# Gates behind the attention by tanh, one request for the Ln/Exp table moved, and a longer planned trip for the recurrence's first unit

## The chip, the cores and the metric

The kernel runs on one core of a Trainium2 chip. The metric is the device time of one launch in microseconds; of several runs the median counts. The core's engines are TensorE (PE; PEld are its weight loads), VectorE (DVE), ScalarE (ACT), GpSimd (POOL) and SyncE (SP), which here issues DMAs.

## The reference

One block of a hybrid model on a sequence of 1024 rows and 1024 columns in fp32: a modulated RMS norm, one wide projection, softmax attention with forget gates (8 heads of 64) beside an RWKV-7 recurrence (8 heads of 64), both weighted by sigmoid gates, an output projection, a second norm, a convolutional FFN (2816) and a last norm.

```python
def token_mixer(u, w_in, fox_b_f, fox_w_out, rwkv_mu, ...):
    proj = u @ w_in
    p_fox, p_rwkv, p_gate = _split(proj, (FOX_COLS, RWKV_COLS, GATE_COLS))
    ...
    o_fox = fox_attention(to_heads(q), to_heads(k), to_heads(v), log_f)
    o_rwkv = rwkv7_time_mix(p_rwkv, ...)
    gate_fox, gate_rwkv = jnp.split(jax.nn.sigmoid(p_gate), N_BRANCHES, axis=-1)
    merged = gate_fox * (o_fox @ fox_w_out) + gate_rwkv * (o_rwkv @ rwkv_w_out)
    return merged @ w_o

def reference(x, c, ...):
    mod = jax.nn.silu(c) @ w_mod[l] + b_mod[l]
    shift1, scale1, gate1, shift2, scale2, gate2 = jnp.split(mod, N_MOD, axis=-1)
    u = modulate(rms_norm(h, ln1_g[l]), shift1, scale1)
    h = h + gate1[:, None, :] * token_mixer(u, ...)
    u = modulate(rms_norm(h, ln2_g[l]), shift2, scale2)
    h = h + gate2[:, None, :] * conv_ffn(u, ...)
    return rms_norm(h, final_g)
```

## The kernel before, in words

Every fp32 operand of a product is split into a high and a low part (`hi_in`, `lo_in`, `u_hi`, `u_lo`), and a product is the sum of three: high by high, low by high, high by low. ScalarE casts the high part, VectorE or GpSimd subtracts for the low one. A projection of 128 columns is two halves (`hf`) of the 1024 rows, each of 3 x 8 matmuls of 128 x 512.

The program has these stages. The *start* squares and transposes `x` (`xt`), sums the modulation from the rows of `w_mod` (`wm`) and makes `u`. Then come low-rank products (*lora*) and the first projections. The *recurrence* goes over 8 units (pair of heads `p`, half `hf`): a preparation (`pre`) inverts small triangular matrices on VectorE (rows `t` and `E`), and a main part (`main`) turns the result `TT` into `X`, multiplies (`xi`, `zi`) and passes a state `S` through eight chunks, each by a TensorE product `sp` and a VectorE scaling. The *attention* follows (`lg` logits, `P` probabilities, `tp` their transpose, `th` and `tl` its parts, `ov` the product with the values); its results are `fx0` (high) and `fx1` (low). Then come the *branch* products (`br`, x = 0 from attention and 1 from recurrence, with weights `raw_br`, `hi_br`, `lo_br`), multiplied by the gates (`g`) on VectorE, the output projection (`wo`), the second norm (`norm2`, once for each half of the rows) and the FFN. During `br`, VectorE also adds up two more modulation vectors from `wm` tiles (`acc3`, `acc4`) and splits the recurrence's results (`rk_raw`) into high and low.

TensorE's order is written by a planner, `Weave`: it keeps a clock `now` from the modelled cost of each matmul, runs chains that yield times to wait, and fills the gaps with steps of projections from a queue: `qk`, `v`, `rkv` and last the 16 gates (`gt`, `gs`). While the attention runs, DVE's and ACT's orders are written out as well; elsewhere the scheduler of the language orders them. Gates taken up before the attention run through `gate_steps` in the form Abs, Exp, Ln, a subtraction and Exp. Gates taken up in it (`weave.late` is 1) run through `late_gate` and `gate_out`, which use 0.5 tanh(0.5 x) + 0.5 and the PSUM tile `rk_ps`; what is left in the queue when `weave.late` is 2 runs behind the attention in the form of `gate_steps` again. The `big` PSUM pool has 2 banks, a pool of loaded weights (`raw`) 2 tiles; `br` goes round 4 banks.

For the first unit, `ready` is the planner's time at which the inverse is back from VectorE and two DMAs: `now` plus 47500 ns; the other units have 38500. `main` waits for `ready - 1500` before it lays out the transposes of X.

`use_ln_exp(after)` asks ScalarE to load the table set that holds Ln and Exp, and with `after` it is ordered behind that instruction; without it, nothing ties it to a place. `rms_rstd` (L292, L293) is an Ln and an Exp.

Of the kernel before, what the change touches and what calls it, by code (L numbers as in the profile page):

```python
# [11 lines left out]
AF = mybir.ActivationFunctionType  # L12
# [123 lines left out]
def hybrid_block(ctx: ExitStack, tc: tile.TileContext, a, out):  # L136
    nc = tc.nc
    weave = Weave()
# [43 lines left out]
    epsr = cp.tile([128, 4], F32, name="epsr")  # L182
# [20 lines left out]
    def use_ln_exp(after=None):  # L203

        i = nc.scalar.preload_act_table_set("natural_log_exp_and_others")
        if after is not None:
            tc.add_manual_dep(i.ins, after.ins.name, NOSYNC)


    d_gate = dr.tile([16, 128, S], F32, name="d_gate")  # L210
# [41 lines left out]
    marks = {}  # L252
# [26 lines left out]
    def gemm_steps(ps, w, x, cs, nk=KT, w0=0, by_kt=False):  # L279
        (wh, wl), (xh, xl) = w, x  # L280
        order = [(i, kt) for i in range(3) for kt in range(nk)]
        if by_kt:
            order.sort(key=lambda o: o[1])
        for n, (i, kt) in enumerate(order):
            ww, xx = ((wh, xh), (wh, xl), (wl, xh))[i]
            k0 = (w0 + kt) * 128
            mm(ps, ww[:, k0 : k0 + 128], xx[:, kt, cs], start=n == 0, stop=n == len(order) - 1)
            yield
# [32 lines left out]
    def gate_steps(w, i, pps, ptag, pool, tag):  # L321
        if weave.late == 1:
            yield from late_gate(w, i)
            return
        for hf in range(2):
            cs = slice(hf * NH, hf * NH + NH)
            ps = pps.tile([128, NH], F32, tag=ptag, name=f"gt{i}_{hf}")
            yield from gemm_steps(ps, w, u, cs)

            g = pool.tile([128, NH], F32, tag=tag, name=f"gs{i}_{hf}")  # L330
            nc.scalar.activation(g, ps, AF.Abs)
            nc.scalar.activation(g, g, AF.Exp, scale=-1.0)
            nc.scalar.activation(g, g, AF.Ln, bias=1.0)
            stt(g, ps, 0.0, g, op0=ALU.min, op1=ALU.subtract)
            nc.scalar.activation(g, g, AF.Exp)
            nc.sync.dma_start(d_gate[i, :, cs], g)
# [3 lines left out]
    with ExitStack() as es:  # L340
# [7 lines left out]
        def gen(name):  # L348
            return pr.tile([128, NH], F32, tag="gen", name=name)
# [407 lines left out]
        def pre(k, p, hf):  # L757

            n = f"{p}_{hf}"
            cs = slice(hf * NH, hf * NH + NH)  # L760
# [5 lines left out]
            def chunk_tile(nm, bufs, *dims):  # L766
                return rw.tile([128, *dims], F32, tag=nm, name=f"{nm}{n}", bufs=bufs)
# [46 lines left out]
            for c0 in range(0, NCU, 4):  # L814
                ps = [gen(f"p1_{n}{h}{c0}") for h in range(2)]
# [15 lines left out]
            M32 = chunk_tile("M32", 1, 32, 32)  # L831
            for g in range(4):
                nc.sync.dma_start(M32[g * 32 : g * 32 + 32, :, :], sm.rearrange("h c b s t -> (h c b) s t"))
            ready = weave.now + (47500 if k == 0 else 38500)
            TT = chunk_tile("TT", 2, NCU, CH)
            weave.spawn(inverse(n, M32, TT, chunk_tile, tmp), 8500)

# [12 lines left out]
            ps = [gen(f"tb{n}{h}") for h in range(2)]  # L850
# [144 lines left out]
        for i in range(16):  # L995
            weave.add(lambda i=i: w_in(26 + i), lambda w, i=i: gate_steps(w, i, pb, "big", gsp, "sp0"))
# [4 lines left out]
        def pre_chain():  # L1001
            for k, (p, hf) in enumerate(order):
                while got[p, hf] < 3:
                    weave.step()
                yield from pre(k, p, hf)
                if p < 3:
                    weave.first.extend(rkv_items(p + 1, hf))
                yield 0
# [43 lines left out]
    with tc.manual_schedule(engines={mybir.EngineType.DVE, mybir.EngineType.Activation}):  # L1052
# [170 lines left out]
        def late_gate(w, i):  # L1223
            for hf in range(2):
                cs = slice(hf * NH, hf * NH + NH)
                yield from gemm_steps(rk_ps, w, u, cs)
                weave.hold = weave.now + 700
                pending.append((i, hf))
                weave.spawn(gate_out(i, hf, cs), 260)
                yield  # L1230

        def gate_out(i, hf, cs):

            g = gsp.tile([128, NH], F32, tag="sp0", name=f"gs{i}_{hf}")
            nc.scalar.activation(g, rk_ps, AF.Tanh, scale=0.5)
            weave.hold = weave.use("ACT", weave.now, 480) + 210
            nc.scalar.activation(g, g, AF.Identity, scale=0.5, bias=epsr[:, 3:4])
            weave.use("ACT", weave.now, 480)
            nc.sync.dma_start(d_gate[i, :, cs], g)
            pending.remove((i, hf))  # L1240
            return
            yield

        def drain():
            begun = weave.cur
            while pending or (weave.cur is begun and begun is not None):
                yield 300
# [2 lines left out]
        weave.run([a_chain(), t_chain(), s_chain()])  # L1250
        weave.late = 2
        weave.run([drain()])
    use_ln_exp()
    es.close()
    pz = ctx.enter_context(tc.tile_pool(name="pz", bufs=1, space=PS))

    def bank(k, name):
        return pb.tile([128, NH], F32, tag="big", name=name) if k > 5 else pz.tile([128, NH], F32, tag=f"p{k}", name=name)
# [33 lines left out]
    br_open(0, 1)  # L1292
    while weave.step():
        pass
    u_st.close()
    ww_st.close()
    pools["m"] = ctx.enter_context(tc.tile_pool(name="sm", bufs=1, side="right", reuse_waits="tile"))
# [75 lines left out]
    for x in range(2):  # L1373
        for n in range(8):
            if x or n:
                k = 8 * x + n + 1
# [299 lines left out]
    ps = {t: [bank(k, f"wo{t}_{c}") for c, k in enumerate(ks)] for t, ks in enumerate(((0, 5), (6, 7), (1, 2)))}  # L1676
# [12 lines left out]
    def wo_do(t, k):  # L1689
        ps = [bank(k + c, f"wo{t}_{c}") for c in range(2)]  # L1690
        for kt in range(KT):
            wo_mm(t, kt, ps)
        return ps

    ps = wo_do(3, 3)
# [5 lines left out]
    ps = wo_do(4, 0)  # L1701
# [11 lines left out]
    for t, k in ((5, 2), (6, 6), (7, 4)):  # L1713
        ps = wo_do(t, k)
# [223 lines left out]
    for s, k in enumerate(ORDER):  # L1938
        ps = banks[4:] if k in (7, 4, 2) else banks[0:4]
# [109 lines left out]
```

## Time and profile before

| | us |
|---|---|
| median of 3 runs | 1674.13 |
| lowest and highest run | 1671.78, 1674.92 |
| profiled execution | 1671.68 |
| its span, first to last instruction | 1669.9 |

The mean granted TensorE clock was 0.989. Stages by their times in the trace: start to 60, lora and first projections to 215, first unit of the recurrence to 262, the other units to 620, attention to 824.6, then gate 15 and, from 835.5, `br` (to 923), output projection, second norm and FFN to the end. In the rows of the trace a line has start, duration, engine, source line, operation, written tile <- read tiles, shape, and in brackets how long the engine had stood idle and on what it waited. L144 is the helper through which all matmuls go. TensorE's last `ov` ends at 822.80.

### The profile page before, as it was taken

The numbers are of one execution on the slowest core, as the hardware profiler recorded it, in microseconds if no ns is written. First come the engines' busy times: TensorE is split into PE (matmuls) and PEld (weight loads), VectorE is DVE, ScalarE is ACT, GpSimd is POOL, SyncE is SP. The second block draws the span as 40 slices with busy tenths as digits, with TensorE's granted clock in tenths as the row PEclk, the third lists the DMA queues.
The fourth block names the chain that finished last, engine by engine and source line by source line (L and its number), as shares of the span: only waits on it lengthen the run. The fifth ranks groups of instructions, "written<-read, shape, count | busy, mean of one in ns | idle before, by whom it ended". The sixth has DMA issues, their size and how long they took to land.

```text
span 1669.9 us, 25913 instructions
## 1 busy us (share of the span) xinstructions
PE 1617.1 (97%) x9722; PEld 1322.9 (79%) x9722; DVE 1208.5 (72%) x2357; ACT 814.8 (49%) x1475; POOL 136.2 (8%) x169
## 2 busy tenths in 40 slices
PE   6899999999999999999999999999999999999998
PEld 4677877787987777787788888888888888888886
DVE  5786787887876636777578445897777777786677
ACT  6463343534355556666533244654444444455455
POOL 0010101211111020222122000000000000000000
PEclk7899999999999999999999999999999999999999
DMA  8497745543343237443387420143323323574463
GB/s 334 136 326 223 186 125 134 130 113 94 105 118 94 87 110 172 127 140 99 117 288 262 171 77 38 64 132 108 101 95 104 111 95 107 194 271 153 129 211 108
DMA packets 121853, 241.70 MB, mean 145 GB/s; under 512 B 39816, under 2 KB 48320, under 8 KB 121728
## 3 DMA queue, kind: packets, MB, share of 16 engines
q1 hardware_dynamic: 112896, 220.94, 41.1%
q0 software_dynamic: 7600, 17.25, 3.8%
q10 hardware_dynamic: 1232, 1.86, 0.4%
q8 instruction: 76, 1.25, 0.3%
q14 instruction: 49, 0.40, 0.1%
HBM read 174.43 MB, written 65.56 MB: 144 GB/s over the span
## 4 chain that ended last, share of the span: by engine, by line
PE 80%; DVE 10%; ACT 5%; DMA 2%; issue 2%; SPq 0%; ACTq 0%; DVEq 0%
PE X L144 13%; PE D L144 13%; PE gt L144 7%; PE Y L144 6%; PE ps_rkv L144 6%; PE br L144 5%; PE wo L144 5%; PE qk L144 4%; PE W L144 3%; PE v L144 3%; PE rk_ps L144 2%; DVE nm L1090 1%; PE low L144 1%; PE ov L144 1%; PE sp L144 1%
## 5 line engine op out<-in xcount | busy, mean ns | idle before, releaser
L144 PE MATMUL D<-op,op 128*128 128x512 f32 x924 | 209.8, 389 | 0.0
L144 PEld LDWEIGHTS D<-op,op 128*128 128x128 f32 x924 | 173.3, 188 | 36.3 <-DVE op L1312 0.3
L144 PE MATMUL X<-T_m,S 128*128 128x512 f32 x440 | 107.4, 390 | 0.1
L144 PEld LDWEIGHTS X<-T_m,S 128*128 128x128 f32 x440 | 82.4, 188 | 18.3 <-ACT T_m L1737 0.7
L1311 ACT CAST op<-g 128x512 fp32r<-128x512 f32 x77 | 47.8, 621 | 73.8 <-PE D L144 47.6
L1312 DVE TENSOR_TENSOR op<-g,op 128x512 fp32r<-128x512 f32 x77 | 53.0, 688 | 41.5 <-ACT op L1311 41.5
L268 DVE TENSOR_TENSOR lo_in<-raw_in,hi_in 128x512 fp32r<-128x512 f32 x96 | 65.9, 724 | 23.5 <-ACT hi_in L263 12.2
L1548 DVE SCALAR_TENSOR_TENSOR c<-ab,vec,c 128x512 f32<-128x512 f32 x88 | 65.9, 750 | 19.5 <-ACT c L1551 17.9
L263 ACT CAST hi_in<-raw_in 128x1024 fp32r<-128x1024 f32 x48 | 50.2, 1049 | 46.5 <-PE ps_rkv L144 27.0
L1512 DVE TENSOR_TENSOR S<-ur,S 128x512 fp32r<-128x512 f32 x66 | 45.4, 690 | 35.4 <-ACT S L1508 35.2
L1163 DVE TENSOR_TENSOR tl<-tp,th 128x512 fp32r<-128x512 f32 (+1 forms) x80 | 50.4, 632 | 27.9 <-ACT th L1158 27.2
L1508 ACT CAST S<-ur 128x512 fp32r<-128x512 f32 x66 | 41.1, 623 | 55.6 <-DVE ur L1501 30.6
L1512 DVE TENSOR_TENSOR A<-ur,A 128x512 fp32r<-128x512 f32 x64 | 44.0, 687 | 31.2 <-ACT A L1508 31.0
L738 DVE TENSOR_TENSOR t<-E,M 128x60 f32<-128x60 f32 (+24 forms) x248 | 55.8, 225 | 10.9 <-DMA M<-sm 4.6
L144 PE MATMUL Y<-T_h,A 128*128 128x512 f32 x264 | 63.5, 389 | 0.0
L144 PE MATMUL Y<-T_h,S 128*128 128x512 f32 x264 | 63.3, 389 | 0.0
L742 DVE TENSOR_TENSOR E<-E,t 128x60 f32<-128x60 f32 (+24 forms) x248 | 56.8, 229 | 5.8
L144 PE MATMUL X<-B_b,A 128*128 128x512 f32 x252 | 60.8, 390 | 0.0
L1099 ACT ACTIVATE P<-lg,nm 128x896 f32<-128x896 f32 (+3 forms) x64 | 47.5, 743 | 27.0 <-DVE nm L1090 24.7
L144 PE MATMUL W<-B_f,A 128*128 128x512 f32 x252 | 60.6, 389 | 0.0
L144 PEld LDWEIGHTS Y<-T_h,A 128*128 128x128 f32 x264 | 49.6, 188 | 10.4
L144 PEld LDWEIGHTS Y<-T_h,S 128*128 128x128 f32 x264 | 49.5, 188 | 10.3
(486 smaller groups left out, 4062.7 us busy)
## 6 DMA issues: line engine op xcount, KB each, us to landing
raw_in<-in_w_in SPq DMA_DIRECT2D x50, 512.0 KB
wm<-in_w_mod SPq DMA_DIRECT2D x48, 512.0 KB
ur<-in_w_up SPq DMA_DIRECT2D x44, 512.0 KB
g<-d_g SPq DMA_DIRECT2D x35, 512.0 KB
d_g<-gs SPq DMA_DIRECT2D x44, 256.0 KB
d_g<-c SPq DMA_DIRECT2D x33, 256.0 KB
d_st<-qh SPq DMA_DIRECT2D x64, 128.0 KB
d_gate<-gs SPq DMA_DIRECT2D x32, 256.0 KB
```

The costliest lines, as they stand in the source:

```text
L144: weave.last = nc.tensor.matmul(o, lhsT, rhs, start=start, stop=stop, skip_group_check=more)
L263: nc.scalar.copy(hi, raw)
L268: nc.vector.tensor_tensor(lo[:, c : c + NH], raw[:, c : c + NH], f32(hi[:, c : c + NH]), op=ALU.subtract)
L738: i = tt(tv, E32[:, 0:J, s : s + 1].to_broadcast([128, J, W]), M32[:, s : s + 1, s + 1 : 32].to_broadcast([128, J, W]), op=ALU.mult)
L742: tt(E32[:, 0:J, s + 1 : 32], E32[:, 0:J, s + 1 : 32], tv, op=ALU.add)
L1099: nc.scalar.activation(e[:, 0:n], lg[:, 0:n], AF.Exp, bias=nm[:, 0:1], accum_out=total)
L1163: tt(tl[:, 0:w], tp[:, 0:w], f32(th[:, 0:w]), op=ALU.subtract)
L1311: nc.scalar.copy(hi, src)
L1312: tt(lo, src, f32(hi), op=ALU.subtract)
L1508: nc.scalar.copy(hi, src)
L1512: tt(lo, src, f32(hi), op=ALU.subtract)
L1548: stt(c, ab[:, x + hf * NH : x + hf * NH + NH], V("conv_w", 22 * x + i), c, op0=ALU.mult, op1=ALU.add)
```

## The change

The diff has four parts. `gate_steps` gets a tanh branch for `weave.late` 2, the same arithmetic as in `gate_out`. The first unit's `ready` goes from 47500 to 51500 ns ahead. The bare `use_ln_exp()` behind the attention is taken out, and one is put behind the loop that empties the queue, ordered behind the last gate's second activation, which `gate_out` and the new branch note in `marks["gate"]`.

```diff
--- before.py
+++ after.py
@@ -328,6 +328,11 @@
             yield from gemm_steps(ps, w, u, cs)
 
             g = pool.tile([128, NH], F32, tag=tag, name=f"gs{i}_{hf}")
+            if weave.late:
+                nc.scalar.activation(g, ps, AF.Tanh, scale=0.5)
+                marks["gate"] = nc.scalar.activation(g, g, AF.Identity, scale=0.5, bias=epsr[:, 3:4])
+                nc.sync.dma_start(d_gate[i, :, cs], g)
+                continue
             nc.scalar.activation(g, ps, AF.Abs)
             nc.scalar.activation(g, g, AF.Exp, scale=-1.0)
             nc.scalar.activation(g, g, AF.Ln, bias=1.0)
@@ -831,7 +836,7 @@
             M32 = chunk_tile("M32", 1, 32, 32)
             for g in range(4):
                 nc.sync.dma_start(M32[g * 32 : g * 32 + 32, :, :], sm.rearrange("h c b s t -> (h c b) s t"))
-            ready = weave.now + (47500 if k == 0 else 38500)
+            ready = weave.now + (51500 if k == 0 else 38500)
             TT = chunk_tile("TT", 2, NCU, CH)
             weave.spawn(inverse(n, M32, TT, chunk_tile, tmp), 8500)
 
@@ -1234,7 +1239,7 @@
             g = gsp.tile([128, NH], F32, tag="sp0", name=f"gs{i}_{hf}")
             nc.scalar.activation(g, rk_ps, AF.Tanh, scale=0.5)
             weave.hold = weave.use("ACT", weave.now, 480) + 210
-            nc.scalar.activation(g, g, AF.Identity, scale=0.5, bias=epsr[:, 3:4])
+            marks["gate"] = nc.scalar.activation(g, g, AF.Identity, scale=0.5, bias=epsr[:, 3:4])
             weave.use("ACT", weave.now, 480)
             nc.sync.dma_start(d_gate[i, :, cs], g)
             pending.remove((i, hf))
@@ -1250,7 +1255,6 @@
         weave.run([a_chain(), t_chain(), s_chain()])
         weave.late = 2
         weave.run([drain()])
-    use_ln_exp()
     es.close()
     pz = ctx.enter_context(tc.tile_pool(name="pz", bufs=1, space=PS))
 
@@ -1292,6 +1296,7 @@
     br_open(0, 1)
     while weave.step():
         pass
+    use_ln_exp(marks["gate"])
     u_st.close()
     ww_st.close()
     pools["m"] = ctx.enter_context(tc.tile_pool(name="sm", bufs=1, side="right", reuse_waits="tile"))
```

What this does to the order of the instructions: ScalarE's first rows before. L1249 asks for the attention's set and L205 is `use_ln_exp` or the sigmoid's request; both have risen to the head of the program. L436 squares `x`.

```order
L1249 ACT_TABLE_LOAD
L205 ACT_TABLE_LOAD
L200 ACT_TABLE_LOAD
L200 ACTIVATE sc_91<-vec_72 128x8
L205 ACT_TABLE_LOAD
L436 ACTIVATE acc1_142,ssq_139<-xt0_145 128x1024
L436 ACTIVATE acc1_142,ssq_139<-xt1_147 128x1024
```

And now (the lines behind the edits have grown by 5):

```order
L1254 ACT_TABLE_LOAD
L200 ACT_TABLE_LOAD
L200 ACTIVATE sc_91<-vec_72 128x8
L205 ACT_TABLE_LOAD
L441 ACTIVATE acc1_142,ssq_139<-xt0_145 128x1024
L441 ACTIVATE acc1_142,ssq_139<-xt1_147 128x1024
```

One of the four loads ahead of the squares is gone. Further on, ScalarE at the end of the attention and the beginning of `br` before; L1235 and L1237 are the late gate, L331 to L335 gate 15:

```order
L1216 CAST fx03_6863<-o31_8684 128x512
L1235 ACTIVATE gs14_1_9115<-rk_ps_6896 128x512
L1285 CAST hi_br00_9141<-raw_br00_9139 128x512
L1237 ACTIVATE gs14_1_9115<-gs14_1_9115,epsr_76 128x512
L1285 CAST hi_br01_9149<-raw_br01_9147 128x512
L331 ACTIVATE gs15_0_9178<-gt15_0_9120 128x512
L332 ACTIVATE gs15_0_9178<-gs15_0_9178 128x512
L333 ACT_TABLE_LOAD
L333 ACTIVATE gs15_0_9178<-gs15_0_9178 128x512
L335 ACT_TABLE_LOAD
L335 ACTIVATE gs15_0_9178<-gs15_0_9178 128x512
L1353 CAST rk00_m0_9234<-rk_raw00_9321 128x512 x2
```

And now:

```order
L1221 CAST fx03_6934<-o31_8755 128x512
L1289 CAST hi_br00_9202<-raw_br00_9200 128x512
L1289 CAST hi_br01_9210<-raw_br01_9208 128x512
L1240 ACTIVATE gs15_1_9180<-rk_ps_6967 128x512
L1242 ACTIVATE gs15_1_9180<-gs15_1_9180,epsr_76 128x512
L205 ACT_TABLE_LOAD
L1289 CAST hi_br02_9279<-raw_br02_9277 128x512
L1358 CAST rk00_m0_9234<-rk_raw00_9321 128x512 x2
```

Gate 15 is now the late gate, and one load stands behind its second activation. Behind this, the loads of L292 and L293 in both calls of `norm2` are gone as well; the whole program has 9 table loads instead of 17.

On TensorE, gate 15's 48 matmuls (`gt15`) are gone from between the last late gate and `br`: the queue has run one gate further ahead everywhere, so that gates 0 to 9 stand before the attention (0 to 8 earlier) and 10 to 15 in it. Twelve of the last gate's (four of low by high, eight of high by low) now stand between the last `ov` and `br`.

VectorE in the first unit, around the transposes of X (STREAM_TRANSPOSE) and `v10`, whose source bank `ps_rkv90` TensorE takes next. Before:

```order
L268 TENSOR_TENSOR lo_in17_2055<-raw_in17_2052,hi_in17_2054 128x512 x2
L879 STREAM_TRANSPOSE X0_0_1627<-TT0_0_1445 32x256 x2
L363 SCALAR_TENSOR_TENSOR v10_1626<-ps_rkv90_1896,omu_81,sh_rkv90_2047 128x512
L738 TENSOR_TENSOR t320_1_1960<-E320_1_1958,M320_1_1853 128x31
L359 COPY sh_rkv11_2377<-pv1r_1816 128x1
L742 TENSOR_TENSOR E320_1_1958<-E320_1_1958,t320_1_1960 128x31
```

And now:

```order
L268 TENSOR_TENSOR lo_in17_2055<-raw_in17_2052,hi_in17_2054 128x512 x2
L368 SCALAR_TENSOR_TENSOR v10_1626<-ps_rkv90_1896,omu_81,sh_rkv90_2047 128x512
L743 TENSOR_TENSOR t320_1_1960<-E320_1_1958,M320_1_1853 128x31
L364 COPY sh_rkv11_2359<-pv1r_1816 128x1
L747 TENSOR_TENSOR E320_1_1958<-E320_1_1958,t320_1_1960 128x31
L784 SCALAR_TENSOR_TENSOR cum1_0_2061<-cst2_122,cum1_0_2061 128x512
L743 TENSOR_TENSOR t320_1_1960<-E320_1_1958,M320_1_1853 128x30
L747 TENSOR_TENSOR E320_1_1958<-E320_1_1958,t320_1_1960 128x30
L743 TENSOR_TENSOR t320_1_1960<-E320_1_1958,M320_1_1853 128x29
L747 TENSOR_TENSOR E320_1_1958<-E320_1_1958,t320_1_1960 128x29
L743 TENSOR_TENSOR t320_1_1960<-E320_1_1958,M320_1_1853 128x28
L884 STREAM_TRANSPOSE X0_0_1627<-TT0_0_1445 32x256 x2
```

The transposes have moved behind `v10`, the scan `cum`, a copy and seven rows of the second unit's inverse. On TensorE, `xi0_0`, which reads X, stands behind 21 matmuls of `qk6_1` instead of 4. Between the first two states of this unit, `S0_00` and `S0_01`, VectorE has, before:

```order
L796 TENSOR_TENSOR bk1_0_2143<-kr1_0_2141,en1_0_2136 128x8x64
L799 TENSOR_SCALAR al1_0_2063<-al1_0_2063,vec_72,oka_89 128x512
L738 TENSOR_TENSOR t320_1_1960<-E320_1_1958,M320_1_1853 128x49
L800 TENSOR_TENSOR al1_0_2063<-al1_0_2063,k10_1625 128x512
L742 TENSOR_TENSOR E320_1_1958<-E320_1_1958,t320_1_1960 128x7x7
L268 TENSOR_TENSOR lo_in21_2328<-raw_in21_2325,hi_in21_2327 128x512 x2
L801 TENSOR_TENSOR bk1_0_2143<-al1_0_2063,en1_0_2136 128x8x64
L805 SCALAR_TENSOR_TENSOR ksq1_0_2309<-r10_1624,vec_72,al1_0_2063 128x512
L738 TENSOR_TENSOR t320_1_1960<-E320_1_1958,M320_1_1853 128x42
L363 SCALAR_TENSOR_TENSOR k11_2041<-ps_rkv51_2225,omu_81,sh_rkv51_2321 128x512
L939 TENSOR_SCALAR S0_01_2345<-sp0_0_2265,pcd0_0_1285 128x64
```

and now:

```order
L801 TENSOR_TENSOR bk1_0_2106<-kr1_0_2104,en1_0_2099 128x8x64
L804 TENSOR_SCALAR al1_0_2063<-al1_0_2063,vec_72,oka_89 128x512
L747 TENSOR_TENSOR E320_1_1958<-E320_1_1958,t320_1_1960 128x8x3
L805 TENSOR_TENSOR al1_0_2063<-al1_0_2063,k10_1625 128x512
L743 TENSOR_TENSOR t320_1_1960<-E320_1_1958,M320_1_1853 128x16
L806 TENSOR_TENSOR bk1_0_2106<-al1_0_2063,en1_0_2099 128x8x64
L810 SCALAR_TENSOR_TENSOR ksq1_0_2340<-r10_1624,vec_72,al1_0_2063 128x512
L747 TENSOR_TENSOR E320_1_1958<-E320_1_1958,t320_1_1960 128x8x2
L268 TENSOR_TENSOR lo_in3_2366<-raw_in3_2363,hi_in3_2365 128x512 x2
L743 TENSOR_TENSOR t320_1_1960<-E320_1_1958,M320_1_1853 128x8
L368 SCALAR_TENSOR_TENSOR r11_2040<-ps_rkv11_2261,omu_81,sh_rkv11_2359 128x512
L944 TENSOR_SCALAR S0_01_2376<-sp0_0_2296,pcd0_0_1285 128x64
```

The last row of each is `S0_01`; ahead of it the rows are partly others, eleven now and ten before. In `br`, VectorE before, from the last `rk` split on (L1333 sums a `wm` tile, L1366 multiplies a product by its gate):

```order
L1354 TENSOR_TENSOR rk11_m7_9241<-rk_raw21_9466,rk10_m5_9239 128x512 x2
L1333 SCALAR_TENSOR_TENSOR acc3_9242<-wm3_3_9290,sc_91,acc3_9242 128x1024
L1366 TENSOR_TENSOR mg0_m9_9227<-g0_2_9283,br2_00_9341 128x512
L1366 TENSOR_TENSOR mg1_m13_9231<-g0_2_9283,br2_01_9355 128x512
L1333 SCALAR_TENSOR_TENSOR acc3_9242<-wm3_4_9335,sc_91,acc3_9242 128x1024
L1366 TENSOR_TENSOR mg0_m9_9227<-g0_3_9331,br3_00_9389 128x512
```

And now:

```order
L1359 TENSOR_TENSOR rk11_m7_9241<-rk_raw21_9466,rk10_m5_9239 128x512 x2
L1338 SCALAR_TENSOR_TENSOR acc3_9242<-wm3_2_9287,sc_91,acc3_9242 128x1024
L1338 SCALAR_TENSOR_TENSOR acc3_9242<-wm3_3_9290,sc_91,acc3_9242 128x1024
L1338 SCALAR_TENSOR_TENSOR acc3_9242<-wm3_4_9335,sc_91,acc3_9242 128x1024
L1371 TENSOR_TENSOR mg0_m9_9227<-g0_2_9283,br2_00_9341 128x512
L1371 TENSOR_TENSOR mg1_m13_9231<-g0_2_9283,br2_01_9355 128x512
```

The sums over the `wm` tiles 2, 3 and 4 now stand ahead of the multiply of `br2_00`; before, tile 2 came further ahead, tile 3 directly before it and tile 4 behind `br2_01`.

## The prediction

> **What bounds the kernel now.** I read the page's busy times and slices first, then TensorE's waits, then windows by stage, and last the timeline around the four places that the change touches. Busy times, and TensorE by fortieths of the span:
>
> ```profile
> PE 1617.1 (97%) x9722; PEld 1322.9 (79%) x9722; DVE 1208.5 (72%) x2357; ACT 814.8 (49%) x1475; POOL 136.2 (8%) x169
> PE   6899999999999999999999999999999999999998
> ```
>
> TensorE bounds the kernel nearly everywhere: it is busy for 97% of the span, and every slice behind the second but the last reads 9. A change can only pay where TensorE stands still. The stages (length, busy time of PE, PEld, DVE, ACT, POOL, granted clock, DMA share, GB/s) are the start, lora and the first projections, the first unit of the recurrence, the other units, attention, and all the rest:
>
> ```profile
> 0.00:60.00 60.00, 38.05 (x147) 27.46 (x148) 38.53 (x61) 34.37 (x54) 0.95 (x5) 0.77 0.72 264
> 60.00:215.00 155.00, 152.88 (x791) 120.86 (x790) 115.95 (x220) 73.25 (x113) 18.49 (x24) 1.00 0.74 226
> 215.00:262.00 47.00, 43.90 (x395) 33.64 (x395) 35.91 (x113) 16.35 (x26) 3.68 (x9) 1.00 0.47 130
> 262.00:620.00 358.00, 356.69 (x3525) 289.15 (x3524) 261.13 (x733) 169.42 (x301) 48.15 (x58) 1.00 0.37 106
> 620.00:824.64 204.64, 189.66 (x1124) 160.63 (x1123) 144.71 (x289) 130.24 (x294) 41.45 (x58) 0.98 0.46 129
> 824.64:1669.90 845.26, 835.93 (x3749) 691.12 (x3747) 612.29 (x944) 391.21 (x688) 23.46 (x16) 1.00 0.42 142
> ```
>
> TensorE idles 22 us at the start, 3.1 in the first unit, 1.3 in the other units, 15.0 in attention. Three of its waits on other engines which the change can touch, in total, times, longest (single ones come below):
>
> ```profile
> PE tr L151 <- DVE xt L442: 9.9, 8, 7.4
> PE lg L144 <- ACT P L1099: 5.6, 10, 1.5
> ...
> PE sp L144 <- DVE S L939: 1.5, 3, 1.0
> ```
>
> **The change, part by part.** The order of the changed kernel shows that no gate is left behind the attention: gates 0 to 9 stand ahead of it, 10 to 15 in it, so the new tanh branch is never entered. Gate 15's 48 matmuls move forward, and twelve of the last gate's matmuls now stand directly before `br`. These 48 run from 824.64 to 835.52 in the rows of the seam below, 10.9 us or 0.227 each; the number of TensorE's instructions stays the same, so they change place and cost nothing. What can gain or lose is waiting.
>
> *Second rstd of the second norm* (norm2 of the lower half). ScalarE loads a table for Ln and another for Exp, and TensorE waits for the diagonal made of the result:
>
> ```profile
> 1024.10 2.96 PE L144 MATMUL W<-B_f,A 128*128 128x512 f32 x12
> 1025.48 1.28 ACT L292 ACT_TABLE_LOAD   x1
> 1026.77 0.30 ACT L292 ACTIVATE ssq<-ssq,epsr 128x4 f32<-128x4 f32 x1
> 1027.09 1.28 ACT L293 ACT_TABLE_LOAD   x1
> 1028.62 0.87 DVE L1415 TENSOR_SCALAR dg<-cst,ssq 128x128 f32<-128x128 f32 x4 [2.96 <-ACT ssq L293]
> 1028.96 3.84 PE L144 MATMUL tr<-dg,h_sb 128*128 128x128 f32 x32 [1.90 <-DVE dg L1415]
> ```
>
> With the common table in place both loads go: 2 x 1.28 = 2.57 us, more than the 1.90 that TensorE waits. The first quarter of the diagonal is then ready at 1028.96 - 2.57 = 1026.39, before TensorE is free at 1024.10 + 2.96 = 1027.06. Gain: the whole wait, **-1.9**. In the first half's norm and at gate 15 the same loads lie under running matmuls, so there they are worth 0. [...]
>
> *The start.* The bare request for the common table stood at the head of ScalarE's program, where nothing uses it before the Sigmoid table replaces it. Below it stand the first and the last of the first four squares of x, and two windows:
>
> ```profile
> 2.04 1.28 ACT L205 ACT_TABLE_LOAD   x1
> 6.14 1.06 ACT L436 ACTIVATE acc<-xt 128x1024 f32<-128x1024 f32 x1
> 9.68 1.06 ACT L436 ACTIVATE acc<-xt 128x1024 f32<-128x1024 f32 x1
> 2.00:8.50 6.50, 2.08 (x6) 2.08 (x7) 0.63 (x6) 6.39 (x9) 0.00 (x0) 1.00 1.03 360
> 18.00:19.00 1.00, 1.00 (x8) 0.79 (x8) 0.00 (x0) 0.81 (x2) 0.00 (x0) 1.00 0.00 0
> ```
>
> That load goes, so the squares, which ran without a gap from 6.14, may start 1.28 us sooner. The last row says that the DMA stands still around 18 us, because its buffers come free only when the transposes of x have run: what moves x forward also moves the transfers behind it. Bounds: -1.28, and 0 if x lands no earlier than it was used. Four x tiles of 512 KB at the 360 GB/s of 2.0 to 8.5 us take 5.8 us, from 2.0 to 7.8 at the earliest, and the first `wm` tiles share the way; the last square would start at 9.68 - 1.28 = 8.40. It nearly fits; I take **-0.9**, nearer to the full load than to 0.
>
> *The first unit* (plan 4 us longer). VectorE's rows in 222 to 252 us, and TensorE's behind them:
>
> ```profile
> 223.72 0.43 DVE L879 STREAM_TRANSPOSE X<-TT 32x256 f32<-32x256 f32 x1 [3.54 <-DMA TT<-se]
> 225.71 1.19 PE L144 MATMUL qk<-u_hi,hi_in 128*128 128x512 f32 x4 [1.46 <-DVE v L363]
> 226.03 0.19 DVE L738 TENSOR_TENSOR t<-E,M 128x31 f32<-128x31 f32 x1 [0.37 <-issue]
> 231.03 1.07 PE L144 MATMUL zi<-TT,X 32*32 32x32 f32 x32 [0.55 <-ACT X L886]
> 251.08 0.33 PE L144 MATMUL sp<-S,Mt 64*64 64x64 f32 x4 [0.95 <-DVE S L939]
> ```
>
> Before, VectorE waits 3.54 us for a DMA ahead of X's transposes, and `v` queues behind them, whose PSUM bank TensorE needs for `qk`: 1.46 lost. Now `v` stands ahead and the transposes follow ten rows later, so that wait goes. In its place: the `t` behind `v` cannot run before 226.0 (its mask), a scan and seven small rows follow, so X is turned near 229.4; TensorE gets to `xi` after 21 matmuls at about 229.0 and waits some 0.5, and some 0.75 for the bank that `ql` frees. Between the first two states S, VectorE has eleven rows of about 5.3 us (at the durations of the same kinds before; it had ten), while TensorE has 14 matmuls between (3.2): wait 1 to 2, before 0.95 at that point. Old waits 1.46 + 0.55 + 0.95 = 2.96, new about 2.2: **-0.8**, bounds -2.5 (all cover holds) and +1.7 (the S wait is 4).
>
> *Other units*: the filler order shifts, but TensorE waits only 1.3 us in 358: **0**, plus or minus 1.
>
> *End of attention.* The last `w_in` load and split (gate 15's) leave it for an earlier, dense place:
>
> ```profile
> 803.82 1.29 DVE L268 TENSOR_TENSOR lo_in<-raw_in,hi_in 128x512 fp32r<-128x512 f32 x2 [2.07 <-ACT hi_in L263]
> 801.73:813.91 12.18, 10.93 (x61) 8.61 (x59) 9.80 (x21) 8.17 (x17) 0.00 (x0) 1.00 0.14 44
> ```
>
> VectorE stood 2.07 us waiting for ScalarE's half of that split and then worked 1.29 on it, with the softmax rows behind. TensorE lost 1.25 us in this window. Most of it goes: **-1.0** (bounds -2 and 0).
>
> *The seam into `br`.* Gate 15 was cover for the last head's split, for `br`'s weights and for the loads behind:
>
> ```profile
> 822.80 2.00 PE L144 MATMUL rk_ps<-u_hi,lo_in 128*128 128x512 f32 x8
> 824.64 1.98 PE L144 MATMUL gt<-u_hi,hi_in 128*128 128x512 f32 x8
> 835.52 1.98 PE L144 MATMUL br<-fx,hi_br 128*128 128x512 f32 x8
> 824.50 0.69 DVE L1218 TENSOR_TENSOR fx<-o,fx 128x512 fp32r<-128x512 f32 x1 [0.69 <-ACT fx L1216]
> 826.03 2.54 POOL L1286 TENSOR_TENSOR lo_br<-raw_br,hi_br 128x512 fp32r<-128x512 f32 x2 [27.31 <-ACT hi_br L1285]
> 847.04 2.30 DVE L1333 SCALAR_TENSOR_TENSOR acc<-wm,sc,acc 128x1024 f32<-128x1024 f32 x1
> 829.00:835.50 6.50, 6.50 (x30) 5.40 (x29) 1.94 (x3) 5.06 (x6) 0.00 (x0) 1.00 0.98 317
> 842.50:845.00 2.50, 2.50 (x12) 2.07 (x12) 1.11 (x2) 2.50 (x6) 0.93 (x1) 1.00 0.84 172
> wm<-in_w_mod SPq DMA_DIRECT2D x48, 512.0 KB
> ```
>
> Call the end of the last `ov` T0 (822.80 before). Twelve matmuls now stand behind it (2.7 us). `fx13` was ready at T0 + 2.4; `br`'s first four products use `fx0`, so it is needed near T0 + 3.6. The low weights, needed after eight products at T0 + 4.5, need a ScalarE cast (now ahead of the gate's Tanh) and 1.27 on POOL: T0 + 3.8. Both fit. The loads have 10.9 us less lead. VectorE's row has three sums over `wm` ahead of the fifth product's multiply, whose bank the ninth product needs 2.7 + 8 x 2.73 = 24.5 us behind T0. About 6.0 MB have to land by then: five `wm`, four `rk_raw` and one `g` of 512 KB, three `raw_br` and a gate's store of 256. At the 317 GB/s of 829 to 835.5 that takes 18.9 us, then up to 2.30 for the sum (1.28 unstretched) and 0.69 for the multiply: T0 + 22. It fits by some 2.5. I take **+0.2** (0 to +2). The one load of the common table falls behind the last gate's Identity, under `br`'s products, whose next cast is not due for some 5 us: 0.
>
> Sum: -1.9 - 0.9 - 0.8 + 0 - 1.0 + 0.2 = **-4.4 us**. The profiled execution took 1671.68 us (span 1669.9 and 1.8 around it) and becomes 1667.3; the three runs have a median of 1674.13, 2.4 above it, so against the median it is 1669.7. That is -0.26%. Two tenths of a per cent, 3.35 us, is what I count as distinguishable from no change.
>
> **The rivals.** *The first unit eats its own gain*: S is late by 4 us instead of 1 to 2, since VectorE works through the same number of long rows with less matmul cover; +1.7 instead of -0.8, sum -1.9, **1672.2**. For it: 3.2 us of cover against 5.3 us of rows; against it: TensorE comes later to that place. *Only norm and start pay* (the attention's softmax row waits on ScalarE anyway, ten times in 5.6 us, and the first unit comes out even): -1.9 - 0.9 = -2.8, **1671.3**. *More than forecast*: all four gains at their lower bounds, -1.9 - 1.28 - 2.5 - 2 = -7.7, **1666.4**; the waits are in the trace, but not all can go at once. *Slower*: `br` starves. At the 172 GB/s of 842.5 to 845 the 6.0 MB take 34.9 us, the multiply of the fifth product ends 2 us later near T0 + 36.9, and TensorE stands 12.4 us at the ninth product: with the other terms' -4.6, +7.8, **1681.9**. It makes the kernel slower once that stall passes 4.6 + 3.35 = 8 us, at a rate under 6.0 / 30.5 = 197 GB/s. For it: ten microseconds of lead are gone and the sums stand in a fixed order; against it: 317 GB/s before, when more was asked for.
>
> **How the numbers follow.** Forecast 0.42; more than forecast 0.17: faster 0.59. First unit 0.20, only norm and start 0.12: within 0.2% 0.32. Starving 0.09: slower 0.09. The range runs from 1665 (the larger gain and the runs' spread of 1.5 either way) to 1675 (first unit, with the same spread), which leaves out mostly the slower case; the forecast alone spans 1667.5 to 1671.
>
> **What would show it.** Right: no wait of `tr` on `dg`, no table load from the last gate to the FFN's activation but one; first square near 4.9 and first transposes 0.9 us sooner; no `qk` wait on `v` near 225; `sp` waits on S under 2.2 us in the first unit; `br` beginning 2.7 us behind the last `ov`, without a gap and dense. Wrong: a wait of over 3 us of `sp` on S, of `br` on a multiply or its weights, or squares that wait for x.

## The result and the profile after

The changed kernel is slower: 1689.93 us median of 6 runs (1686.46 to 1691.92) against 1675.57 (1671.78 to 1677.63, 6 runs), a ratio of 1.0085, interval 1.0067 to 1.0102, which is some 14 us. The forecast was 4.4 us faster. The profiled execution has a span of 1689.9 us, 20.0 more than before; that is more than the 14, because the profiled execution of before lies 3.9 under the median of its runs and that of the changed kernel 1.7 over. TensorE on the page of the changed kernel, busy time, fortieths and granted clock:

```profile
PE 1625.2 (96%) x9722; PEld 1331.5 (79%) x9722; DVE 1209.3 (72%) x2357; ACT 804.3 (48%) x1467; POOL 138.7 (8%) x169
PE   5899999999989899999999999999999999999998
PEclk8899999999999899999999999999999999999999
```

Two slices in the middle have left 9, and one has a lower clock; both lie in the recurrence. The same number of matmuls is busy for 8.1 us longer, and 11.9 us more are idle. Windows cut at the same events, from the second unit's first product `p` (the first unit's main part comes behind it) to the attention's first `lg`, and from there to the last `ov`; first of before, then of the changed kernel:

```profile
200.94:628.66 427.72, 423.31 (x4081) 341.41 (x4080) 315.32 (x894) 198.86 (x348) 60.76 (x79) 1.00 0.40 114
628.66:822.80 194.14, 179.16 (x1078) 151.99 (x1077) 139.28 (x280) 122.98 (x282) 35.34 (x49) 0.98 0.44 120
```

```profile
202.31:660.11 457.80, 441.24 (x4128) 356.53 (x4128) 318.44 (x897) 203.75 (x357) 61.09 (x79) 0.98 0.38 108
660.11:851.80 191.69, 176.52 (x1075) 150.29 (x1073) 138.95 (x278) 121.74 (x281) 35.57 (x49) 0.99 0.42 118
```

The recurrence is 30.1 us longer. Gate 9's 48 matmuls, which moved in here, are 10.9 of these; the other 19.2 are 12.2 us more idle time (16.56 against 4.41) and 7.0 of slower matmuls (17.9 more busy, less 10.9). The difference by places:

| from | to | before | after | without the moved gate |
|---|---|---|---|---|
| 0 | second unit's first `p` | 200.94 | 202.31 | +1.4 |
| second unit's first `p` | first `lg` | 427.72 | 457.80 | **+19.2** |
| first `lg` | last `ov` | 194.14 | 191.69 | -2.4 |
| last `ov` | first `br` | 12.72 | 2.74 | +0.9 |
| first `br` | first `wo` | 87.21 | 87.20 | 0.0 |
| first `wo` | second norm's last diagonal used | 106.23 | 107.35 | +1.1 |
| that | end | 640.94 | 640.81 | -0.1 |

The +1.4 of the first row can't be read as an effect: the very first `p` starts anywhere from 165.4 to 169.8 us in the eleven profiles of this document.

What TensorE waits for in the recurrence (215 to 650 us of the changed kernel: total, times, longest), and then the rows of the sixth and the seventh unit (X for the sixth in the last row):

```profile
PE xi L144 <- DVE X L884: 12.3, 6, 5.0
PE sp L144 <- DVE S L944: 3.5, 3, 1.8
PE ps_rkv L144 <- DVE ql L394: 0.7, 1, 0.7
500.65 0.28 PE L144 MATMUL xi<-X,E 32*32 32x32 f32 x2 [4.87 <-DVE X L884]
501.67 1.06 PE L144 MATMUL xi<-X,E 32*32 32x32 f32 x30 [0.74 <-DVE X L884]
557.85 0.28 PE L144 MATMUL xi<-X,E 32*32 32x32 f32 x2 [4.98 <-DVE X L884]
558.81 1.05 PE L144 MATMUL xi<-X,E 32*32 32x32 f32 x30 [0.69 <-DVE X L884]
500.08 0.43 DVE L884 STREAM_TRANSPOSE X<-TT 32x256 f32<-32x256 f32 x1 [2.55 <-DMA TT<-se]
```

In the sixth and the seventh unit TensorE stands 5.6 and 5.7 us before `xi`, because X, the turned inverse, is not there; before, no `xi` waited at all. X itself waits for the DMA that brings the inverse back, and this was issued late. The trip runs from the mask (M, counted from the first of its four DMAs) over 62 rows on VectorE to the inverse's way out (se). The DMA queue's rows, first of before for the same two units, then after:

```profile
425.78 1.71 SPq L833 DMA_DIRECT2D M<-sm  x4
459.68 2.61 SPq L745 DMA_DIRECT2D se<-E  x4
477.80 1.71 SPq L833 DMA_DIRECT2D M<-sm  x4
507.58 3.27 SPq L745 DMA_DIRECT2D se<-E  x4
```

```profile
445.45 0.32 SPq L838 DMA_DIRECT2D M<-sm  x1
494.40 2.52 SPq L750 DMA_DIRECT2D se<-E  x4
503.47 1.71 SPq L838 DMA_DIRECT2D M<-sm  x4
551.63 2.52 SPq L750 DMA_DIRECT2D se<-E  x4
```

It took 33.9 and 29.8 us before, and takes 49.0 and 48.2 now. The planner allots every unit but the first 38.5 us, whatever else VectorE has to do.

Why it got long is read from VectorE's groups within the trip. The splits of weights in the sixth and the seventh unit's trip before (32 and 28 us from the landed mask on), and in the sixth unit's now (46 us):

```profile
L268 DVE TENSOR_TENSOR lo_in<-raw_in,hi_in 128x512 fp32r<-128x512 f32 x4 | 2.6, 684 | 0.0
L268 DVE TENSOR_TENSOR lo_in<-raw_in,hi_in 128x512 fp32r<-128x512 f32 x6 | 3.9, 688 | 0.4 <-PE ps_rkv L144 0.2 <-ACT hi_in L263 0.2
```

```profile
L268 DVE TENSOR_TENSOR lo_in<-raw_in,hi_in 128x512 fp32r<-128x512 f32 x12 | 10.1, 869 | 0.1
```

In the new order all six projections of the last pair of heads fall into the sixth unit's trip: twelve halves of splits, where this trip had four before and the seventh's six, and beside them six shifted sums, where the two had none and three. In the seventh unit the rows of the inverse start late. First row `t` before; after, the gate's subtraction ahead of it in the queue, and the first `t`:

```profile
482.94 0.18 DVE L738 TENSOR_TENSOR t<-E,M 128x31 f32<-128x31 f32 x1
```

```profile
507.57 0.69 DVE L339 SCALAR_TENSOR_TENSOR gs<-gt,gs 128x512 f32<-128x512 f32 x1 [5.24 <-ACT gs L338]
517.73 0.18 DVE L743 TENSOR_TENSOR t<-E,M 128x31 f32<-128x31 f32 x1
```

Its mask was issued by 505.2 (503.47 + 1.71), but ahead of the inverse's first row VectorE has a gate's subtraction, ahead of which it stands 5.24 us, and the sixth unit's own rows (QA, Wt, Zt, Mt), ahead of which it waits 4.7 us in all for products behind the late X. So the first delay hands on a part of the second: 12.5 us from mask to first row, 3.4 before. These 9.1 us are half of the 18.4 by which the seventh trip grew; the other half lies between its rows, where the order has put gates and the eighth unit's preparation.

### The profile page after: what moved, and what is told of

Read it like the earlier page. It is cut to its first block, busy times and chain, and to the rows that moved or that the text cites. A ratio compares the mean times of both kernels' runs of the same rounds, so it can differ in the third digit from the quotient of the medians.

```text
span 1689.9 us, 25922 instructions
## 1 busy us (share of the span) xinstructions
PE 1625.2 (96%) x9722; PEld 1331.5 (79%) x9722; DVE 1209.3 (72%) x2357; ACT 804.3 (48%) x1467; POOL 138.7 (8%) x169
## 4 chain that ended last, share of the span: by engine, by line
PE 83%; DVE 9%; ACT 4%; DMA 2%; issue 1%; SPq 0%; ACTq 0%; DVEq 0%
PE X L144 13%; PE D L144 12%; PE gt L144 7%; PE ps_rkv L144 6%; PE Y L144 6%; PE wo L144 5%; PE br L144 5%; PE qk L144 5%; PE W L144 3%; PE v L144 3%; PE rk_ps L144 2%; PE sp L144 1%; PE low L144 1%; DVE nm L1095 1%; PE ov L144 1%
## 5 line engine op out<-in xcount | busy, mean ns | idle before, releaser
L1553 DVE SCALAR_TENSOR_TENSOR c<-ab,vec,c 128x512 f32<-128x512 f32 x88 | 65.9, 750 | 19.5 <-ACT c L1556 17.9
L743 DVE TENSOR_TENSOR t<-E,M 128x60 f32<-128x60 f32 (+24 forms) x248 | 60.3, 243 | 15.6 <-DMA M<-sm 9.8
```

The source lines that it names most:

```text
L743: i = tt(tv, E32[:, 0:J, s : s + 1].to_broadcast([128, J, W]), M32[:, s : s + 1, s + 1 : 32].to_broadcast([128, J, W]), op=ALU.mult)
L1553: stt(c, ab[:, x + hf * NH : x + hf * NH + NH], V("conv_w", 22 * x + i), c, op0=ALU.mult, op1=ALU.add)
```

## The experiments

**Only the trip.** The kernel before with one number changed; TensorE's order is exactly that of the changed kernel, the table loads are those of before.

```diff
-            ready = weave.now + (47500 if k == 0 else 38500)
+            ready = weave.now + (51500 if k == 0 else 38500)
```

> The kernel before with the 51500 alone; TensorE's order is that of the changed kernel, the table loads are those of before. Theory A (the longer planned trip reorders the recurrence, and X is late in later units): slower than before by 14 to 18 us, with some 12 us of xi waiting for X, and the 1.9 us wait on dg back. Theory B (the table request and the tanh edits cost the time): within 3 us of before, xi waits under 1 us.

Measured 1691.45 us against 1676.33, ratio 1.0098 (1.008 to 1.0115). The waits of this kernel:

```profile
PE xi L144 <- DVE X L879: 12.2, 6, 5.1
PE tr L144 <- DVE dg L1415: 1.9, 1, 1.9
```

Theory A holds: the whole loss comes with this one number, and the 1.9 us on `dg` are back.

**All but the trip.**

```diff
-            ready = weave.now + (51500 if k == 0 else 38500)
+            ready = weave.now + (47500 if k == 0 else 38500)
```

> The changed kernel with 47500 again: all of the tanh and table edits, TensorE's order exactly as before, gate 15 behind the attention but by tanh. Theory A: 1.9 us (the dg wait) to 3 us faster than before, xi waits none. Theory B: 12 us or more slower. The blind forecast's start term would add -0.9; if x lands no earlier, nothing.

Measured 1673.73 us against 1676.33, ratio 0.9992 (0.9978 to 1.0007). No `xi` waits, no wait on `dg`. Theory B falls. The gain that theory A expected here, 0.1 to 0.2%, lies inside the interval and so does none.

**The planned trip by steps.** The changed kernel with 49500 and with 53500 for the first unit.

> The changed kernel with the first unit's trip at 49500. If a later first X is what costs (each us of plan pushes the others), it stands half way: about 7 us over the kernel with 47500 and half the xi wait. If the number only picks one of many orders, it can be anything from -2 to +15, and the xi waits need not lie between.

> The same at 53500. If the cost grows with the planned trip: over 20 us above before, xi waits over 14. If the number only picks an order: anything from -2 to +20, tied to the xi and S waits that come out.

Ratios 1.0085 (1.0063 to 1.0107, four runs) and 1.0104 (1.006 to 1.0147, two runs). The waits, first of 49500:

```profile
PE xi L144 <- DVE X L884: 11.4, 5, 5.0
```

```profile
PE xi L144 <- DVE X L884: 11.2, 4, 5.1
```

The cost doesn't grow with the number. All three values above 47500 have the same two waits of 5.5 to 5.7 us in the sixth and seventh unit, so the step lies between 47500 and 49500. The three orders are not the same, but any two of them agree in about nine tenths of the places of TensorE's 9722 matmuls: the number picks an order, and the three picked here are much alike.

**The splits off VectorE.** The changed kernel, with the low parts of the last pair's weights and of the early gates' weights on GpSimd.

```diff
+POOLED = {f"in{i}" for i in (15, 19, 23, *range(26, 42))}
+        half = nc.gpsimd if weave.late == 0 and name in POOLED else nc.vector
         for c in range(0, n, NH):
-            nc.vector.tensor_tensor(lo[:, c : c + NH], ...)
+            half.tensor_tensor(lo[:, c : c + NH], ...)
```

> The changed kernel, with the low-part subtraction of the last pair's six projection weights and of the gates' weights ahead of the attention on GpSimd instead of VectorE; TensorE's order is the same. Theory A1 (X is late in the sixth and seventh unit because VectorE is full between the mask's landing and the end of the inverse): the xi waits of 11.3 us there fall under 4, and the time by 8 to 15 us against the changed kernel. Theory A2 (the trip is set by the DMAs and the fixed chain of the inverse): xi waits stay above 9 us, the time moves under 3 us.

Measured 1695.53 us, ratio 1.0118 (1.0099 to 1.0137): not faster. The trace, the sixth unit's trip, three waits, and the seventh unit's trip with its first row `t`:

```profile
453.84 0.33 SPq L840 DMA_DIRECT2D M<-sm  x1
491.92 2.52 SPq L752 DMA_DIRECT2D se<-E  x4
482.84 0.33 PE L145 MATMUL sp<-S,Mt 64*64 64x64 f32 x4 [2.87 <-DVE S L946]
501.05 0.50 PE L145 MATMUL mu<-Mtr,blk_r 128*128 128x512 f32 x1 [2.01 <-POOL Mtr L732]
566.66 0.26 PE L145 MATMUL xi<-X,E 32*32 32x32 f32 x2 [3.90 <-DVE X L886]
516.60 2.56 SPq L840 DMA_DIRECT2D M<-sm  x4
526.38 0.18 DVE L745 TENSOR_TENSOR t<-E,M 128x31 f32<-128x31 f32 x1
560.22 2.52 SPq L752 DMA_DIRECT2D se<-E  x4
```

With the splits gone the sixth unit's trip is 38.1 us and its `xi` waits no more, so A1's mechanism holds for that unit. Its numbers did not come: `xi` still waits 6.6 us in all, between A1's 4 and A2's 9, and the time did not fall. A state S (2.87) and a product that waits for GpSimd (`mu`, 2.01) take the place. The seventh unit shows how much the first delay hands on: without it the first row comes 7.2 us behind the mask instead of 12.5, yet the trip is still 43.6 us and `xi` waits 4.4 there instead of 5.7. The waits moved; the time did not improve.

**The gate without VectorE.** The changed kernel, with a shorter form of the early gates.

```diff
-            nc.scalar.activation(g, ps, AF.Abs)
-            nc.scalar.activation(g, g, AF.Exp, scale=-1.0)
+            nc.scalar.activation(g, ps, AF.Exp, scale=-1.0)
             nc.scalar.activation(g, g, AF.Ln, bias=1.0)
-            stt(g, ps, 0.0, g, op0=ALU.min, op1=ALU.subtract)
-            nc.scalar.activation(g, g, AF.Exp)
+            nc.scalar.activation(g, g, AF.Exp, scale=-1.0)
```

> The changed kernel with the early gates as Exp, Ln, Exp on ScalarE alone (three activations for five, and no VectorE step); TensorE's order is the same. Theory A1 for the seventh unit (VectorE stood 5.2 us behind a gate's subtraction during that inverse): the xi wait of 5.7 us in the seventh unit falls under 3, and the total by 3 to 8 us; the sixth unit's 5.6 may stay. Rival A2: the xi waits stay above 10 us in total and the time moves under 3 us.

Measured 1689.82 us, ratio 1.0095 (1.0075 to 1.0114).

```profile
500.67 0.28 PE L144 MATMUL xi<-X,E 32*32 32x32 f32 x2 [4.83 <-DVE X L882]
556.55 0.28 PE L144 MATMUL xi<-X,E 32*32 32x32 f32 x2 [3.64 <-DVE X L882]
```

The seventh unit's first wait falls only from 4.98 to 3.64 (with the second one from 5.7 to 4.3, not under 3), all `xi` waits to 10.8, and the time does not fall: what the rival A2 said. The gate's row was a small part. What else fills the seventh trip is read from the traces above, and no run took all of it away.

**Longer trips for the other units** (44500 for 38500, the first at 51500).

> The changed kernel with the other seven units' planned trip at 44500 instead of 38500 (the first stays at 51500). Theory A1 (TensorE gets to X before the real trip ends, which took 48 us from the mask to the inverse's end in the sixth and seventh unit): TensorE arrives 6 us later in each unit, with fillers between; xi waits fall from 12.3 us to under 4 and the time by 6 to 14 us against the changed kernel. Rival A2 (whatever the planned trip, the order that comes out is what it is, and a new order has new waits): xi waits above 6 us in other units, or as much waiting elsewhere; time within 4 us of the changed kernel.

Measured 1685.33 us against 1673.65, ratio 1.0082 (1.0052 to 1.0111). Its waits in the recurrence, then the windows of the recurrence and the attention as above, and the first row of `br`:

```profile
PE sp L144 <- DVE S L944: 5.0, 4, 2.3
PE xi L144 <- DVE X L884: 2.9, 3, 2.5
201.12:656.50 455.38, 446.44 (x4176) 360.83 (x4176) 319.30 (x904) 211.27 (x367) 61.50 (x79) 1.00 0.40 114
656.50:843.26 186.76, 169.62 (x1038) 143.80 (x1036) 136.78 (x276) 120.82 (x279) 34.93 (x49) 0.99 0.40 111
845.38 2.08 PE L144 MATMUL br<-fx,hi_br 128*128 128x512 f32 x8 [2.12 <-issue]
```

`xi` waits go from 12.3 to 2.9, as A1 said, and 2.7 of these are in the first unit. The time did not follow: its interval overlaps that of the changed kernel, as A2 said. Its profile, the fastest of the four runs, is 9.2 us longer than that of before, and most of this is idle time in three places: 8.94 us in the recurrence (4.41 before), 17.14 in the attention (14.98), and 2.12 ahead of `br` (none before), where no matmul is left behind the last `ov`, since the queue has run another gate ahead. What the slower runs add is not placed.

**The one-column block dealt out.** In the profile of the changed kernel the granted clock was 0.50 from 960.2 to 964.5 us, behind `mps`, 32 matmuls of one column each in the middle of the output projection. This kernel is the table edits with 47500, and the block spread over the projection (shortened: `spread` is `mod_2()`, opened ahead of the projection and run out behind it):

```diff
-        if kt == 4:
-            for _ in mod_2():
-                pass
+                if t == 0 and kt > 3:
+                    next(spread, None)
```

> As e2, and the 32 one-column mps matmuls of the second norm's modulation are dealt out among the output projection's matmuls instead of standing in one block. Theory C (the block of about 3.5 us counts as idle in some runs and the clock is then halved for some 6 us): no window under 0.97 there, median 1 to 3 us under e2, runs closer together. Rival (the clock falls there for another reason): same clock row, time within 1 us of e2.

Measured 1670.15 us against 1676.33, ratio 0.9967 (0.9952 to 0.9982), and 3.6 us under the same kernel with the block (the two intervals overlap a little, from 0.9978 to 0.9982). Nine us from the block's start, of before, after and the table edits alone; then the same place dealt out, in two windows (granted clock third from the end):

```profile
936.60:945.60 9.00, 9.00 (x57) 7.99 (x56) 0.50 (x3) 0.00 (x0) 0.00 (x0) 1.00 0.23 93
```

```profile
955.62:964.62 9.00, 9.00 (x43) 8.12 (x42) 0.50 (x3) 0.00 (x0) 0.00 (x0) 0.62 0.30 121
```

```profile
937.01:946.01 9.00, 9.00 (x44) 7.98 (x43) 0.50 (x3) 0.00 (x0) 0.00 (x0) 0.65 0.16 67
```

```profile
930.00:939.00 9.00, 9.00 (x50) 7.65 (x48) 3.45 (x5) 1.67 (x2) 0.00 (x0) 1.00 1.01 406
939.00:948.00 9.00, 9.00 (x46) 7.57 (x45) 0.17 (x1) 0.00 (x0) 0.00 (x0) 1.00 0.02 9
```

The clock stayed at 1.00 in both windows, as theory C said; that the block counts as idle was its guess, and no run shows it. The median fell by more than its 1 to 3 us, and the runs did not come closer together (1666.62 to 1675.41).

**Both, and the shorter gate.** The last kernel with the gate form above.

> As e5 (47500, table and tanh edits, mps dealt out), and the early gates as Exp, Ln, Exp on ScalarE alone. Theory (TensorE's order is that of before, its waits in the recurrence are 3 us in all, so less work on VectorE and ScalarE has nothing to give there): as e5, 0.3% under before, within 1 us of it. Rival (VectorE's gate rows delay what TensorE waits for here too): another 2 us or more under e5, waits of sp on S gone.

Measured 1671.27 us against 1675.88, ratio 0.997 (0.9958 to 0.9981): the same as without, and `sp` waits on S for 1.5 us as before, so the rival falls. Both kernels with the block dealt out are 0.3% faster than the one before, and some 20 us faster than the changed one.

## Why the prediction was wrong, step by step

*Other units, "0, plus or minus 1".* This is the step that failed. The argument was that TensorE waited only 1.3 us there; but a wait of the old order is no bound for a new one, and the change rewrote the order of all eight units. I had compared the orders around the first unit and the attention, not the seven units between. Measured: +19.2 for the whole recurrence, some 17 of it in the other units (the first unit's part is worked out below). The late X of the sixth and the seventh unit alone are 11.3 of the 12.2 us more idle time. None of the rivals named it.

*First unit, -0.8.* Wrong in sign. The `qk` wait went as said, and in its place came 1.02 on X, 0.73 on `ql`'s bank and 1.82 on S: 3.6 against 3.0, or +0.6. The sum had no term for the clock, which was 1.00 in this window before and is 0.96 now, by estimate up to 1.9 us (0.04 x 47); with it the unit lies above the upper bound of +1.7:

```profile
215.00:262.00 47.00, 43.43 (x355) 34.11 (x356) 35.72 (x110) 15.18 (x26) 4.53 (x8) 0.96 0.46 126
```

*Start, -0.9.* The load went, x was not there. The first two squares of the changed kernel:

```profile
5.22 1.06 ACT L441 ACTIVATE acc<-xt 128x1024 f32<-128x1024 f32 x1 [0.38 <-DMA xt<-in_x]
7.30 1.06 ACT L441 ACTIVATE acc<-xt 128x1024 f32<-128x1024 f32 x1 [0.94 <-DMA xt<-in_x]
```

The bound 0 was the right end: the fourth square ends no sooner than before.

*Second rstd, -1.9.* Right. The Ln follows its input by 0.23 us, with no load between, and the turn no longer waits:

```profile
1049.09 3.73 PE L144 MATMUL tr<-dg,h_sb 128*128 128x128 f32 x32
```

In the table above it hides behind `mps`: the wait's -1.9 and a rest of +3.0 make +1.1, and the clock of 0.62 over 9 us (shown with the experiment on `mps`) is by estimate worth up to 3.4 (0.38 x 9).

*End of attention, -1.0.* The idle time there is 15.17 us against 14.98 (length less busy): no gain shows. Two profiles can't settle a term of 1.0, though: with TensorE's order of before this idle time is 14.98 to 17.49 us in four profiles. The 2.4 us by which the attention is shorter are 0.9 of matmuls that stand behind its end now, and for the rest faster matmuls (clock 0.99 for 0.98).

*Seam, +0.2.* Right: no wait shows, and the slower rival was the wrong one. (Its transfers are 6.3 MB, not 6.0, since 512 KB are 524,288 bytes; at 317 GB/s that is 19.8 us instead of 18.9, which still fits.) `br` starts 2.74 us behind the last `ov` and takes 87.20 us, as before (row of the changed kernel):

```profile
854.54 1.98 PE L144 MATMUL br<-fx,hi_br 128*128 128x512 f32 x8
```

*The base.* The profile of before is the only one of nine with the block of `mps` in which the clock stayed at 1.00 there; in the other eight it was 0.62 to 0.81. Over 9 us these clocks are by estimate worth 1.7 to 3.4 us (0.19 x 9 and 0.38 x 9), which is likely most of the 3.9 by which it lay under the median; for the runs without a profile it is not shown.

## What to carry to other kernels

When one number feeds a planner, the whole order that comes out has to be compared, not the place that the number is named after: a local look can't bound it. A planner that allots a fixed time to a chain on a shared engine should be held against the longest trip in the trace, and against what else the order puts on that engine meanwhile; there, one late result is a part of what delays the next chain behind it (here some 5 of the 18 us by which that chain's trip grew). Taking work off such an engine did not pay here in two tries, with the order of the engine it serves as it was.

## What the runs showed of the hardware

Behind the two late X of the changed kernel the granted clock fell, so that these waits cost more than their length. It was 1.00 in the 5.8 us ahead of the first of them (490.00 to 495.78), and in the 7 to 8 us behind each:

```profile
500.65:507.73 7.08, 6.34 (x44) 4.82 (x44) 1.28 (x3) 2.59 (x5) 0.00 (x0) 0.53 0.50 135
557.85:566.00 8.15, 7.46 (x86) 6.00 (x88) 2.82 (x6) 2.91 (x8) 0.00 (x0) 0.54 0.73 210
```

Behind these stretches it was 1.00 again (508 to 520 and 566 to 575 us). By estimate from the two rows the busy time loses up to 6.4 us (6.34 x 0.47 and 7.46 x 0.46), most of the 7.0 us of slower matmuls in the recurrence. The five other profiles with a wait of 3.6 us or more on X have nine such waits, and behind each the matmuls are slow: in the sixth unit (four waits) the first six `gt` took 2.87 to 2.93 us, while with 53500 the next six took 1.55; in the seventh unit (five waits) a row of `vt` or `at` took 0.42 us, while the same kind took 0.27 in the sixth, 7 to 8 us behind the start of `xi`. With 49500 the granted clock over 7.6 us was 0.56 behind the one and 0.72 behind the other. What length of wait this takes was not measured. What I had not expected is that TensorE need not be idle: behind 32 matmuls of one column in 3.6 to 4.8 us, with TensorE busy throughout by the profile (9.00 of 9.00 us), the clock fell in eight of nine profiles (0.62 to 0.81 over 9 us from the block's start), and in both profiles with these matmuls dealt out it stayed at 1.00 (two windows of 9 us each).
